# Every other weight chunk of the last down projection: low parts by an accumulating DMA in place of a VectorE subtraction

## The chip, the cores and the metric

One core of one Trainium2 chip runs the whole program. The metric is device time in microseconds (us) of one execution, the median of several runs of the same kernel. The core has a matrix engine (TensorE, PE in the rows, with its weight loads as PEld), VectorE (DVE), ScalarE (ACT), GpSimd (POOL), SyncE (SP), and 16 DMA engines that all queues share. SP and ACT hand their transfers to hardware queues (q1 and q10 in the profile); transfers that POOL issues go through a software queue (q0).

## The reference

Two transformer blocks run one after the other on a sequence of 256 positions with 1024 channels, all in float32. The first has a recurrent branch and an attention branch and a feed-forward part with a short convolution; the second has windowed attention, latent attention and a gated feed-forward part. Only the very end of the second block matters here:

```python
    h = rmsnorm_2(x, ffn_norm_g[l])
    x = x + (jax.nn.silu(h @ w_gate[l]) * (h @ w_up[l])) @ w_down[l]
    return rmsnorm_2(x, final_norm_g)
```

The last product, of a 256 x 2816 activation and the 2816 x 1024 matrix `w_down`, is what this document calls the last down projection. The addition of `x`, the final norm and the store follow it.

## The kernel before

**Split products.** Float32 accuracy on TensorE is had by splitting both operands. A value `w` is stored as a high part `wh`, which is `w` rounded to the narrower float32r type, and a low part `wl = w - wh`. A product takes three matmuls: activation high by weight high, activation low by weight high, activation high by weight low.

**Weight chunks.** All weights arrive in chunks of 128 partitions by up to 2048 columns. `produce()` makes one: SP loads it into a tile `wt`, ScalarE copies it into `wh` (the copy rounds), and VectorE subtracts to get `wl`. The pool `wp` has three buffers for each of `wt`, `wh` and `wl`, and `chunk()` keeps production two chunks ahead of use (`LOOK = 2`). From the second block's `w2_ukv` on, a chunk is loaded and split in two halves of 1024 columns (`cuts`), so that each chunk is two loads of 512 KB, two ScalarE copies and two VectorE subtractions.

**The last down projection.** `w2_down` has 11 chunks (d0 to d10 below; in the rows of the trace the digits in a tensor's name are left out, so it shows as in_w_down). Each chunk holds two blocks of 128 input rows (`k`), each 1024 columns wide, so a chunk's first half serves `k = 0` and its second half `k = 1`. Four PSUM banks (`o`, two token halves by two column halves) collect the result. For each chunk, each `k` and each `o` there are three matmuls of 512 columns, two of which read `wh` and the third `wl`: 24 matmuls a chunk. Chunk d9 is held back and done together with d10, bank by bank, so that the banks finish one after the other:

```python
        held += [(o, c, k, W) for k in range(2) for o in range(4)]
        if c == KH - 2:
            continue
        for o, c_, k, (wh, wl) in sorted(held, key=lambda x: x[0] if c == KH - 1 else 0):
```

**Order.** The program's order is not the order of the text. `Scheduler` collects all operations with a modelled cost, and list-schedules them: at each step the engine that can start first takes its available operation of the lowest index, and the result is emitted as one sequence (`emit`, the line 333 that all rows carry). Loads on every queue share one modelled "DMA" engine. The semaphores come from the tile framework: a reader waits for the tile's writer, and a new tile in a buffer waits until the last reader of the old tile is done. So the load of chunk c+3 into a `wt` buffer waits for the last reader of chunk c in that buffer, and the ScalarE copy into `wh` of chunk c waits for the last matmul that reads the `wh` of chunk c-3.

POOL computes nothing in this stage; it issues only five transfers in the whole program, the last two of them `final_g`.

Of the kernel before, what the change touches and what calls it, by code (L numbers as in the profile page):

```python
# [9 lines left out]
F32 = mybir.dt.float32  # L10
F32R = mybir.dt.float32r
BF16 = mybir.dt.bfloat16
AF = mybir.ActivationFunctionType
ALU = mybir.AluOpType
# [321 lines left out]
class Engines:  # L336
# [5 lines left out]
    def act(self, out, in_, func, **kw):  # L342
        n = max(out.n, in_.n)
        cost = (0.053 if in_.tile.psum else 0.093) + n / 1200.0
        cost += 0.09 * sum(isinstance(kw.get(k), View) for k in ("scale", "bias")) + (0.1 if "accum_out" in kw else 0.0)
        return self.sch.add("ACT", self.nc.scalar.activation, cost, (out, in_, func), kw, table=SETS.get(func))
# [16 lines left out]
    def dma(self, queue, out, in_):  # L363
        v = out if isinstance(out, View) else in_
        cost = v.shape[0] * v.n * 4 / 360e3
        self.sch.add(f"DMA", getattr(self.nc, queue).dma_start, cost, (out, in_), {}, lag=1.2)

    def memset(self, out, value):
        self.sch.add("DVE", self.nc.vector.memset, 0.1, (out, value), {})

# [31 lines left out]
def _build(ctx, tc, sch, A, out, order, used):  # L402
# [17 lines left out]
    V = Engines(sch, nc)  # L420
    act = V.act
# [60 lines left out]
    def produce():  # L482
        i = state["next"]
        name, idx = order[i]
        n = A[name].shape[-1]
        wt = wp.tile([P, 2048], F32, tag="wt")
        wh = wp.tile([P, 2048], F32R, tag="wh")
        wl = wp.tile([P, 2048], F32R, tag="wl")


        cuts = [0, n // 2, n] if i < 4 or i >= fine else [0, n]
        for a, b in zip(cuts, cuts[1:]):
            V.dma("sync", wt[:, a:b], A[name][idx][:, a:b])
            act(wh[:, a:b], wt[:, a:b], AF.Copy)
            V.tensor_sub(wl[:, a:b], wt[:, a:b], wh[:, a:b].bitcast(F32))
        ready[i] = (wh, wl)
        state["next"] = i + 1

    def chunk(name, idx):
        i = len(used)  # L500
        used.append((name, idx))
        if order is None:
            t = wp.tile([P, 2048], F32R, tag="wh")
            return t, t
        assert order[i] == (name, idx)
        while state["next"] <= min(i + LOOK, len(order) - 1):
            produce()
        return ready.pop(i)
# [874 lines left out]
```

## Time and profile before

| what | value |
| --- | --- |
| median of 3 runs | 808.87 us (808.72 to 810.1) |
| the profiled execution's own time | 809.6 us |
| its span, first to last instruction | 807.8 us |
| granted TensorE clock, mean | 0.999 |
| busy in the span | PE 796.9, PEld 684.3, DVE 598.4, ACT 522.8, POOL 3.0 us |
| all DMA, mean rate over the span | 175 GB/s |

The span is what the profiler's records cover; the execution's own time is a little longer. Engine shares are averages over stages of different kinds. A matmul's recorded duration overlaps with the next one's, so that the pitch between starts, and not the recorded duration, says how long a row of matmuls takes.

### The profile page before, as it was taken

How to read it: one execution, taken by the hardware profiler on the slowest of the kernel's cores; microseconds unless marked ns; L12 is line 12 of the kernel's file. 1: busy time of each engine (PE TensorE's matmuls, PEld its weight loads, DVE VectorE, ACT ScalarE, POOL GpSimd, SP SyncE). 2: the span in 40 equal slices, each digit the busy share in tenths (PEclk: the TensorE clock that was granted, in tenths of full speed). 3: DMA queues.
4: the chain of work that ended last, by engine and by line, in shares of the span. 5: the costliest groups of instructions: out<-in, count | busy, mean ns of one | idle time of the engine just before them, and what ended most of it. 6: DMA issues, size and time to landing. Idle time of an engine off the chain costs nothing.

```text
span 807.8 us, 11604 instructions
## 1 busy us (share of the span) xinstructions
PE 796.9 (99%) x4414; PEld 684.3 (85%) x4414; DVE 598.4 (74%) x999; ACT 522.8 (65%) x898; POOL 3.0 (0%) x9
## 2 busy tenths in 40 slices
PE   9999999999999999999999999999999999999996
PEld 6888888888888888888888888888888888888885
DVE  6777869977779798888656776666789887877443
ACT  7979889955445766666444667766746765555332
POOL 0000000000000000000000000000000000000000
PEclk9999999999999999999999999999999999999999
DMA  8853444565554455444556544423445665565631
GB/s 293 308 195 105 157 162 166 181 209 172 194 200 172 176 185 207 172 176 144 179 181 227 206 162 134 156 87 123 157 157 170 200 203 183 183 194 176 204 104 53
DMA packets 31260, 141.57 MB, mean 175 GB/s; under 512 B 3490, under 2 KB 5284, under 8 KB 23140
## 3 DMA queue, kind: packets, MB, share of 16 engines
q1 hardware_dynamic: 30228, 138.62, 50.6%
q0 software_dynamic: 400, 1.31, 0.5%
q10 hardware_dynamic: 576, 0.89, 0.3%
q8 instruction: 35, 0.57, 0.3%
q14 instruction: 21, 0.17, 0.1%
HBM read 139.76 MB, written 1.05 MB: 174 GB/s over the span
## 4 chain that ended last, share of the span: by engine, by line
PE 95%; ACT 2%; DMA 1%; DVE 1%; SPq 0%; issue 0%; DVEq 0%; ACTq 0%
PE b_banks L333 95%; DMA wt_wp<-in_w_q 1%; DMA u_up<-in_w_k 1%; ACT t_tp L333 1%; ACT wh_wp L333 1%; DVE wl_wp L333 0%; SPq L333 0%; DVE t_tp L333 0%; ACT pr_ap L333 0%; DVE u_up L333 0%; DVE pr_ap L333 0%; ACT k_cp L333 0%; DVEq L1378 0%; DVE k_cp L333 0%; DVE s_sp L333 0%
## 5 line engine op out<-in xcount | busy, mean ns | idle before, releaser
L333 PE MATMUL b_banks<-r_rp,wh_wp 128*128 128x512 f32 x1584 | 549.8, 398 | 0.0
L333 PE MATMUL b_banks<-r_rp,wl_wp 128*128 128x256 f32 x1584 | 414.5, 281 | 0.0
L333 DVE TENSOR_TENSOR wl_wp<-wt_wp,wh_wp 128x1024 fp32r<-128x1024 f32 (+4 forms) x187 | 298.8, 1611 | 79.4 <-ACT wh_wp L333 78.8
L333 PEld LDWEIGHTS b_banks<-r_rp,wh_wp 128*128 128x128 f32 x1584 | 285.6, 188 | 52.1
L333 PEld LDWEIGHTS b_banks<-r_rp,wl_wp 128*128 128x128 f32 x1584 | 298.3, 189 | 17.2
L333 ACT ACTIVATE wh_wp<-wt_wp 128x1024 fp32r<-128x1024 f32 (+4 forms) x187 | 252.1, 1368 | 72.0 <-PE b_banks L333 59.5
L333 ACT ACTIVATE t_tp<-b_banks 128x256 f32<-128x256 f32 (+1 forms) x180 | 68.8, 386 | 154.0 <-PE b_banks L333 153.9
L333 PE MATMUL b_banks<-wh_wp,r_rp 128*128 128x512 f32 (+2 forms) x472 | 146.1, 388 | 0.0
L333 PEld LDWEIGHTS b_banks<-wh_wp,r_rp 128*128 128x128 f32 x472 | 88.0, 188 | 15.9
L333 DVE TENSOR_TENSOR t_tp<-b_banks,t_tp 128x256 f32<-128x256 f32 (+1 forms) x160 | 61.4, 399 | 42.4 <-ACT t_tp L333 40.6
L333 PE MATMUL b_banks<-wl_wp,r_rp 128*128 128x512 f32 (+2 forms) x236 | 91.4, 387 | 0.4 <-DVE wl_wp L333 0.3
L333 PEld LDWEIGHTS b_banks<-wl_wp,r_rp 128*128 128x128 f32 x236 | 44.3, 188 | 9.6 <-DVE wl_wp L333 1.7
L333 DVE TENSOR_TENSOR t_tp<-t_tp,u_up 128x512 f32<-128x512 f32 x50 | 34.2, 686 | 2.3 <-ACT t_tp L333 1.5
L333 ACT ACT_TABLE_LOAD x26 | 33.4, 1283 | 1.2 <-PEq L1372 0.7
L333 DVE TENSOR_TENSOR t_tp<-t_tp,t_tp 128x512 f32<-128x512 f32 (+1 forms) x46 | 25.8, 564 | 5.7 <-ACT t_tp L333 5.3
L333 DVE SCALAR_TENSOR_TENSOR t_tp<-k_cp,k_cp,t_tp 128x256 f32<-128x256 f32 x68 | 28.3, 478 | 0.0
L333 DVE TENSOR_TENSOR r_rp<-t_tp,r_rp 128x512 fp32r<-128x512 f32 x34 | 23.2, 687 | 4.2 <-ACT r_rp L333 3.5
L333 DVE TENSOR_TENSOR u_up<-b_banks,t_tp 128x256 f32<-128x256 f32 x32 | 13.1, 421 | 16.8 <-ACT t_tp L333 16.8
L333 ACT ACTIVATE r_rp<-t_tp 128x512 fp32r<-128x512 f32 x34 | 21.2, 626 | 6.6 <-DVE t_tp L333 6.1
L333 DVE TENSOR_TENSOR u_up<-b_banks,u_up 128x256 f32<-128x256 f32 (+1 forms) x37 | 14.6, 437 | 9.6 <-PE b_banks L333 9.5
L333 ACT ACTIVATE pr_ap<-pr_ap,s_sp 128x128 f32<-128x128 f32 (+1 forms) x48 | 21.3, 447 | 0.0
L333 ACT ACTIVATE r_rp<-u_up,k_cp 128x256 fp32r<-128x256 f32 x32 | 14.9, 500 | 8.5 <-DVE u_up L333 5.2
(93 smaller groups left out, 470.5 us busy)
## 6 DMA issues: line engine op xcount, KB each, us to landing
wt_wp<-in_w_g SPq DMA_DIRECT2D x12, 1024.0 KB, 4.7
wt_wp<-in_w_up SPq DMA_DIRECT2D x11, 1024.0 KB, 4.7
wt_wp<-in_w_gate SPq DMA_DIRECT2D x11, 1024.0 KB, 4.8
wt_wp<-in_w_down SPq DMA_DIRECT2D x16, 704.0 KB, 4.1
wt_wp<-in_w_gate SPq DMA_DIRECT2D x22, 512.0 KB, 4.4
wt_wp<-in_w_up SPq DMA_DIRECT2D x22, 512.0 KB, 4.1
wt_wp<-in_w_down SPq DMA_DIRECT2D x22, 512.0 KB, 4.1
wt_wp<-in_w_x SPq DMA_DIRECT2D x4, 1024.0 KB, 4.8
```

The costliest lines, as they stand in the source:

```text
L333: op.fn(*[get(a) for a in op.args], **{k: get(v) for k, v in op.kw.items()})
```

## The change

The condition picks chunks d1, d3, d5, d7 and d9. For each half of these, ScalarE writes minus the rounded value into `wl` (a second copy, with scale -1), and a DMA issued by GpSimd then adds `wt` into `wl` in place; the VectorE subtraction is gone for them. Chunks with even numbers are made as before. The new operation has a modelled cost and a modelled delay of 2.0 us in the scheduler, on the same modelled "DMA" engine as the loads.

```diff
+    def dma_add(self, out, in_):
+        cost = out.shape[0] * out.n * 4 / 360e3
+        self.sch.add("DMA", self.nc.gpsimd.dma_start, cost, (out, in_), dict(accum_op=ALU.add), lag=2.0)
+
...
             V.dma("sync", wt[:, a:b], A[name][idx][:, a:b])
             act(wh[:, a:b], wt[:, a:b], AF.Copy)
-            V.tensor_sub(wl[:, a:b], wt[:, a:b], wh[:, a:b].bitcast(F32))
+            if name == "w2_down" and idx % 2:
+
+                act(wl[:, a:b], wt[:, a:b], AF.Copy, scale=-1.0)
+                V.dma_add(wl[:, a:b], wt[:, a:b])
+            else:
+                V.tensor_sub(wl[:, a:b], wt[:, a:b], wh[:, a:b].bitcast(F32))
```

## Rows read from the trace of the kernel before

**Rows 1.** The page: busy time of each engine; the chain that ended last.

```profile
PE 796.9 (99%) x4414; PEld 684.3 (85%) x4414; DVE 598.4 (74%) x999; ACT 522.8 (65%) x898; POOL 3.0 (0%) x9
...
PE 95%; ACT 2%; DMA 1%; DVE 1%; SPq 0%; issue 0%; DVEq 0%; ACTq 0%
```

**Rows 2.** The chain of waits from 735 us on: start, length, what.

```profile
734.89 66.72 PE b_banks L333 x303
```

**Rows 3.** Timeline, PE, 741 to 802: start, length, instructions.

```profile
741.59 0.62 PE L333 MATMUL b_banks<-wh_wp,r_rp 128*128 128x512 f32 x2
742.04 0.39 PE L333 MATMUL b_banks<-wl_wp,r_rp 128*128 128x512 f32 x1
...
747.03 0.62 PE L333 MATMUL b_banks<-wh_wp,r_rp 128*128 128x512 f32 x2
...
790.55 0.62 PE L333 MATMUL b_banks<-wh_wp,r_rp 128*128 128x512 f32 x2
...
801.21 0.39 PE L333 MATMUL b_banks<-wl_wp,r_rp 128*128 128x512 f32 x1
```

**Rows 4.** Timeline, ACT, 736 to 787; in brackets idle time before and its releaser.

```profile
736.47 2.00 ACT L333 ACTIVATE wh_wp<-wt_wp 128x1024 fp32r<-128x1024 f32 x2
738.37 0.62 ACT L333 ACTIVATE t_tp<-t_tp 128x512 f32<-128x512 f32 x1
739.01 1.28 ACT L333 ACT_TABLE_LOAD   x1
...
741.09 0.39 ACT L333 ACTIVATE t_tp<-b_banks 128x256 f32<-128x256 f32 x1 [0.59 <-PE b_banks L333]
...
743.96 0.63 ACT L333 ACTIVATE r_rp<-t_tp 128x512 fp32r<-128x512 f32 x1
747.05 2.01 ACT L333 ACTIVATE wh_wp<-wt_wp 128x1024 fp32r<-128x1024 f32 x2 [2.46 <-issue]
...
779.64 2.01 ACT L333 ACTIVATE wh_wp<-wt_wp 128x1024 fp32r<-128x1024 f32 x2 [3.43 <-PE b_banks L333]
785.09 2.01 ACT L333 ACTIVATE wh_wp<-wt_wp 128x1024 fp32r<-128x1024 f32 x2 [3.43 <-PE b_banks L333]
```

**Rows 5.** Timeline, DVE, the subtractions of d3, d9 and d10.

```profile
748.15 2.36 DVE L333 TENSOR_TENSOR wl_wp<-wt_wp,wh_wp 128x1024 fp32r<-128x1024 f32 x2 [1.92 <-ACT wh_wp L333]
...
780.74 2.36 DVE L333 TENSOR_TENSOR wl_wp<-wt_wp,wh_wp 128x1024 fp32r<-128x1024 f32 x2 [3.08 <-ACT wh_wp L333]
786.18 2.36 DVE L333 TENSOR_TENSOR wl_wp<-wt_wp,wh_wp 128x1024 fp32r<-128x1024 f32 x2 [3.08 <-ACT wh_wp L333]
```

**Rows 6.** Tile wt, 742 to 803: durations ns, minimum, median, maximum; landing in us.

```profile
L333 ACT ACTIVATE wh_wp<-wt_wp x18: 1044/1052/1061, 742.1 to 786.1; 128x1024 fp32r<-128x1024 f32 x18
L333 DVE TENSOR_TENSOR wl_wp<-wt_wp,wh_wp x18: 1216/1218/1226, 743.3 to 787.3; 128x1024 fp32r<-128x1024 f32 x18
...
DMA to landing us min/median/max: 3.9/4.1/4.9
```

**Rows 7.** Waits of SP's queue, 717 to 775: total us, times, longest.

```profile
SPq L333 <- DVE wl_wp L333: 50.2, 11, 4.7
```

**Rows 8.** Page and view of DMA issues: count, KB each, median us to landing.

```profile
wt_wp<-in_w_uq SPq DMA_DIRECT2D x4, 288.0 KB, 2.9
...
u_up<-in_final_g POOLq DMA_DIRECT2D x2, 256.0 KB, 3.0
...
u_up<-in_cbsb POOLq DMA_DIRECT2D x1, 256.0 KB, 4.5
```

**Rows 9.** Timeline, POOL: its last transfer.

```profile
560.77 0.54 POOL L333 DMA_DIRECT2D u_up<-in_final_g  x1 [11.30 <-PE b_banks L333]
```

**Rows 10.** Windows: busy PE, PEld, DVE, ACT, POOL; clock, DMA share, GB/s.

```profile
747.00:758.00 11.00, 11.00 (x50) 9.10 (x49) 4.72 (x4) 4.14 (x5) 0.00 (x0) 1.00 0.65 203
...
769.00:780.00 11.00, 11.00 (x50) 9.11 (x49) 4.72 (x4) 4.14 (x5) 0.00 (x0) 1.00 0.48 170
780.00:791.00 11.00, 11.00 (x50) 9.10 (x49) 4.72 (x4) 3.67 (x4) 0.00 (x0) 1.00 0.00 0
```

## The prediction

> **What bounds the kernel now.** I read the page first: PE is busy for 796.9 of 807.8 us, and the chain that ended last is 95% PE [rows 1]. A busy PE is not a PE at its peak, so I then read the chain in order of time: from 734.89 us on, one unbroken piece of 66.72 us of matmuls leads to 801.61, past which only the tail of the final norm is left [rows 2]. No wait for a weight chunk stands in it. The change touches this stretch alone, so the question is whether a low part ever comes late enough to break it.
>
> The PE timeline gives the due times [rows 3]. The last down projection begins at 741.59 with d0, d1 begins at 747.03, so a chunk takes 5.44 us, 0.227 us for each of its 24 matmuls. The third matmul of a chunk is the first that reads `wl`, 0.45 us after the chunk's start (742.04 after 741.59). The second half of `wl` is first read 12 matmuls later, at 2.72 + 0.45 = 3.17 us. For d9, which is interleaved with d10 from 790.55 on, the second half comes after three matmuls only, at 0.68 + 0.45 = 1.13 us.
>
> The ACT and DVE timelines give the times of production. ScalarE's copies for d3 begin at 747.05, with the start of d1; those for d9 at 779.64 and for d10 at 785.09 keep the step of 5.44 us, and the releaser is PE [rows 4]. This is the buffer rule: chunk c waits for the last matmul of c-3, which is the start of c-2. Let T be the start of ScalarE's work for a chunk; its first matmul then comes at T + 10.88. Each of the two copies costs 1.05 us with a pitch of 0.96 (two take 2.01), the first subtraction starts 1.10 after its copy started, and both are done by 750.51, T + 3.46 [rows 4, 5]. VectorE's work is thus ready 7.9 us before its use, and VectorE is idle more than half of this stage, 4.72 us busy in 11 [rows 10].
>
> **The change, part by part.**
>
> *Removed:* ten subtractions of 1218 ns, 12.2 us of VectorE [rows 6]. They end 7.9 us ahead of their use, so their removal gives 0.
>
> *Added on ScalarE:* ten copies of 1.05 us [rows 6]. An odd chunk then occupies ScalarE for about 4 x 0.96 + 0.1 = 3.9 us of its 5.44 instead of 2.0; before d9 and d10 it sat idle for 3.43 us [rows 4]. Cost 0, covered by that idle time. One place is tighter: d1 is made at 736.47, among the work of the gated part. Silu at 738.37 moves by 1.9 us to about 740.3, the table load behind it from 739.01 to 740.9, and the eviction due at 741.09 starts at about 742.4, 1.3 us late, since 0.59 us of idle time is used up [rows 4]. What waits for it: the copies of d2 (from 742.07 to about 743.4; their matmuls start at 752.47, two chunks after 741.59) and the split of the last activation tile (743.96 to about 745.3; only d10 reads it, after 790.55). Cost 0; without that cover it would be 1.3 us.
>
> *Added on POOL and the DMA engines:* ten in-place additions of 512 KB. POOL issued its last transfer at 560.77, in 0.54 us [rows 9]; nothing stands ahead of the additions on its queue, and behind each stands only the next. Order within a chunk: copy, minus-copy, addition, and the same for the second half. The minus-copy ends at the second pitch, so the first addition is issued at about T + 0.96 + 1.10 = T + 2.06 and the second at T + 3.98. Call the time from issue to landing L. Against the due times (T + 10.88 plus 0.45, 3.17, or 1.13):
>
> - first half: L up to 10.88 + 0.45 - 2.06 = 9.27 us (d1, which starts its copies at 736.47 for a first `wl` matmul at 747.48: 8.95);
> - second half: up to 10.07 us;
> - second half of d9: up to 10.88 + 1.13 - 3.98 = 8.03 us, the tightest.
>
> The trace shows no accumulating DMA and no transfer from SBUF to SBUF, so L is bounded by the nearest rows. A 256 KB load from POOL took 3.0 us, and 512 KB from SP in this stage 4.1; on SP 288 KB took 2.9 [rows 6, 8]. From 288 to 512 KB it is 1.2 us, or 2.7 us for each 512 KB more; the POOL path costs 0.3 us above that line. The addition reads two operands: L = 4.1 + 0.3 + 2.7 = 7.1 us, which I take, as an estimate. Lower end: 3.0 us, the POOL row itself. Upper end: the slowest POOL load, 4.5 us for 256 KB [rows 8], for each of the four 256 KB that an addition reads, 18 us. At 7.1 the tightest due time holds with 0.9 us left, the others with 1.9 or more. Cost 0.
>
> What a late addition would cost follows from the same times. A stall in chunk c puts off the start of c+1 and of c+2, while c+2's copies started with c; so the stall is also room for c+2. For one L everywhere, d1, d5 and d9 pay and d3 and d7 do not: (L - 8.95) + (L - 9.27) + (L - 8.03) = 3L - 26.25 us. At the upper end this is 27.8 us, at the lower end nothing. L = 9.3 us is the point from which 0.2% is lost.
>
> Only a page has a price for the addition itself: the Trainium skill, "Collectives: The Full Stack", section "The bandwidth ceiling: the fold count and why AG ≠ RS ≠ AR", puts an add at half the rate of a copy because it reads two sources, at about 31 GB/s a DMA engine for a copy. By that, 16 engines would need an estimated 2.1 us to move 512 KB, and the sum would be 0 as well; no trace here shows it.
>
> *Moved:* the release of `wt`. SP's queue now waits for VectorE's subtractions, 11 times in this stage, 50.2 us [rows 7]; after odd chunks it will wait for the second addition. For odd c the loads of c+3 go out at T + 3.98 + L, about T + 11.1 where it was T + 3.5, and land by about T + 15.7 with two loads in a row. ScalarE wants them at the start of c+1, T + 16.3. So they are just in time, and late loads have another 7.9 us before PE notices. Queued behind them on SP are the loads of c+4, wanted at T + 21.8. Cost 0. With the cover gone (L beyond 13) they would add to the stalls.
>
> **Sum.** 0 against the profiled execution's 809.6 us (span 807.8, 1.8 us around it). That execution lies 0.7 us above the median of 808.87 and inside the runs' 808.72 to 810.1; I predict 808.9. About 0.2%, 1.6 us, is what a measurement of this kernel can tell from no change.
>
> **The rivals.**
>
> *A. The addition takes longer than its room (slower).* Place: the first `wl` matmul of d1 and d5 and the second half of d9. Decides from L = 9.3. If reading and writing back were two POOL transfers in a row at the slowest POOL pace, 4.5 us and 1.4 more (the slope above) for 512 KB, L is 11.8, and 3L - 26.25 gives 9.2 us: 818.0. For it: no row shows such an operation, and POOL loads reached 4.5. Against: the two final_g loads took 3.0 [rows 8], and the margin at my estimate is 0.9 us for d9 and 1.9 or more for the others. Chance 0.10.
>
> *B. The DMA engines become the bound.* From 747 to 758 they were busy 65% at 203 GB/s [rows 10]: 312 GB/s when busy, 1.68 us for 512 KB. From the first addition at 738.5 on, 14 loads (d4 to d10) take 23.5 us, and ten additions that read twice 33.6 us; that ends at 795.6, where the last addition is due at 791.68: 3.9 us, 812.8. Against: the loads stop early, with the share at 0.48 from 769 and 0.00 from 780 to 791 [rows 10], and a busy share counts waiting for HBM too, which a transfer inside SBUF does not have. Chance 0.08.
>
> *C. VectorE holds up POOL's issue.* Were each addition to wait out the pair of subtractions of an even chunk, 2.36 us [rows 5], L would be 9.5 and the time 811.0. Against: the pair for d10 runs from 786.18, when the additions of d9 (issued at about 781.7 and 783.6) are under way. The Trainium skill, "SBUF — State Buffer", section "SBUF: two separate sides", says that GpSimd cannot write descriptors while VectorE runs an operation in a two-port mode. No run here shows this yet. Chance 0.03.
>
> *D. Faster by over 0.2%.* PE would have to run its matmuls closer than 0.227 us because VectorE reads less. In 780 to 791, with no DMA at all, PE did the same 50 matmuls in 11 us as in 747 to 758 [rows 10], so neighbours do not seem to set its pitch. I price it at 2 us, 806.9. Chance 0.04.
>
> **How the numbers follow.** No change: 0.75. A and B and C are slower: 0.21, faster 0.04. The range goes from 807.4, below the runs' lowest by their spread, to 814.0, above B and C; outside it are A and half of D, some 0.12, and a little of the main case.
>
> **What would show it.** Right: VectorE has ten subtractions fewer, ScalarE ten copies more, PE's piece of the chain from 735 on is still about 66.7 us, d1 still follows d0 after 5.44 us, and the additions land within 8.0 us. Wrong: a PE wait released by a POOL transfer on `wl`, first at d1 or in d9's second half; or SP loads that land in more than 6 us and copies of even chunks that wait for them.

## The result, and the profile after

The changed kernel took 816.4 us (median of four runs, 813.91 to 818.02) against 808.93 for the kernel before on the same chip: a ratio of 1.0089, with a 95% interval of 1.0069 to 1.0108. It is slower by 0.9%, where no change was forecast and the range ended at 814.0.

The profiled execution has a span of 815.4 us, 7.6 more than before. The page: busy time by engine, and the chain that ended last; these answer to [rows 1].

```profile
PE 798.3 (98%) x4414; PEld 685.0 (84%) x4414; DVE 586.9 (72%) x989; ACT 532.0 (65%) x908; POOL 11.7 (1%) x19
...
PE 86%; DMA 5%; issue 4%; ACT 2%; DVE 2%; SPq 0%; POOL 0%; DVEq 0%; POOLq 0%; ACTq 0%
```

VectorE did ten instructions fewer and ScalarE ten more, so the change did what it says. But the chain is no longer PE alone. The chain in order of time, which answers to [rows 2], has lost its unbroken piece of matmuls:

```profile
750.81 9.63 DMA wl_wp<-wt_wp
760.44 0.02 SPq L333
760.46 0.03 issue
760.49 6.31 DMA wt_wp<-in_w_down
...
776.88 9.02 DMA wl_wp<-wt_wp
785.91 0.04 issue
785.95 23.21 PE b_banks L333 x94
```

It reads: the second addition of d3 (issued at 750.81) lands after 9.63 us; SP's queue, which stood waiting for it, issues a load; and the first addition of d7 (issued at 776.88) lands after 9.02 us, when PE goes on at once. Between that load's landing (766.8) and 776.88 the chain shows almost nothing but 9.99 us of "issue": it does not follow ScalarE there, whose rows further down fill this gap.

The PE timeline, those matmuls that read `wl`, where a normal step from one to the next is 0.68 us, as in [rows 3]:

```profile
771.06 0.39 PE L333 MATMUL b_banks<-wl_wp,r_rp 128*128 128x512 f32 x1
773.44 0.50 PE L333 MATMUL b_banks<-wl_wp,r_rp 128*128 128x512 f32 x1 [1.54 <-DMA wl_wp<-wt_wp]
774.25 0.39 PE L333 MATMUL b_banks<-wl_wp,r_rp 128*128 128x512 f32 x1
...
781.06 0.39 PE L333 MATMUL b_banks<-wl_wp,r_rp 128*128 128x512 f32 x1
785.95 0.80 PE L333 MATMUL b_banks<-wl_wp,r_rp 128*128 128x512 f32 x1 [4.05 <-DMA wl_wp<-wt_wp]
787.39 0.63 PE L333 MATMUL b_banks<-wl_wp,r_rp 128*128 128x512 f32 x1
788.68 0.63 PE L333 MATMUL b_banks<-wl_wp,r_rp 128*128 128x512 f32 x1
789.70 0.40 PE L333 MATMUL b_banks<-wl_wp,r_rp 128*128 128x512 f32 x1
...
808.76 0.39 PE L333 MATMUL b_banks<-wl_wp,r_rp 128*128 128x512 f32 x1
```

The loss can be added up from these starts. The second half of d5 comes 1.70 us late (771.06 to 773.44 less 0.68) and the step after it is 0.13 too long. The first half of d7 comes 4.21 us late (781.06 to 785.95 less 0.68). Then three steps take 3.75 us where they should take 2.04, 1.71 more. Together 7.75 us. The last `wl` matmul starts at 808.76 instead of 801.21, 7.55 later, though the first, at 741.60, was 0.44 sooner than before; the 0.24 still missing lie mostly at d3, where the two steps that end at 758.81 are too long. The long matmuls behind the second wait are the clock: the window from 780 to 791 below has a mean grant of 0.84, and within it the microsecond from 786.90 on has 0.50, the lower level, 1.2 GHz. There a matmul that takes 0.39 us elsewhere took 0.63, and a step 1.29 instead of 0.68.

Windows, with the columns of [rows 10]:

```profile
747.00:758.00 11.00, 11.00 (x49) 8.83 (x48) 2.36 (x2) 6.08 (x7) 1.70 (x2) 1.00 1.03 260
...
780.00:791.00 11.00, 6.95 (x24) 5.33 (x23) 1.82 (x2) 4.27 (x5) 1.72 (x2) 0.84 1.03 224
...
786.90:787.90 1.00, 1.00 (x4) 0.74 (x3) 0.00 (x0) 0.00 (x0) 0.46 (x1) 0.50 1.00 197
```

The DMA engines, busy 65% from 747 to 758 before, are now full there, and again from 780 to 791, where they had nothing to do before. The queues and the issues from 735 to 800 us (packets, MB, share of sixteen engines; count, KB, median us to landing):

```profile
q0 software_dynamic: 1440, 5.24, 42.6%
q1 hardware_dynamic: 2302, 8.38, 39.6%
...
wt_wp<-in_w_down SPq DMA_DIRECT2D x14, 512.0 KB, 6.3
wl_wp<-wt_wp POOLq DMA_DIRECT2D x10, 512.0 KB, 8.3
```

Ten additions took 0.426 x 65 = 27.7 us of all sixteen engines, 2.8 us each. The loads' queue took 25.7 us for 8.38 MB, which is what sixteen loads carry (14 were issued in this window, and what was still under way from before counts too): 1.6 us each, or 22.5 for the 14. A load lands after 6.3 us, not 4.1 [rows 6]. The tile `wl` (durations in ns; landing in us, minimum, median, maximum):

```profile
L333 ACT ACTIVATE wl_wp<-wt_wp x10: 1039/1042/1059, 735.5 to 785.2; 128x1024 fp32r<-128x1024 f32 x10
L333 POOL DMA_DIRECT2D wl_wp<-wt_wp x10: 845/854/899, 736.9 to 786.5; - x10
...
DMA to landing us min/median/max: 5.0/8.3/11.8
```

The waits of SP's queue, which answer to [rows 7], and ScalarE's timeline for d6 and d7:

```profile
SPq L333 <- DMA wl_wp<-wt_wp: 44.6, 5, 11.6
```

```profile
768.12 1.06 ACT L333 ACTIVATE wh_wp<-wt_wp 128x1024 fp32r<-128x1024 f32 x1 [6.78 <-DMA wt_wp<-in_w_down]
773.63 2.01 ACT L333 ACTIVATE wh_wp<-wt_wp 128x1024 fp32r<-128x1024 f32 x2 [4.45 <-DMA wt_wp<-in_w_down]
775.55 1.04 ACT L333 ACTIVATE wl_wp<-wt_wp 128x1024 fp32r<-128x1024 f32 x1
```

ScalarE, which used to wait for PE [rows 4], now waits for loads. The row at 773.63 holds the second half of d6 and the first of d7, in that order: d7 stands behind d6 on ScalarE's queue. Its minus-copy starts at 775.55, its addition goes out at 776.88 and lands at 785.9. SP began no issue between 746.96 and 760.49, and then four loads within 2.3 us, beside the two additions of d5. In the order in which the kernel emits them, these are the first half of d7, both halves of d6 and the second half of d7. The last two, issued at about 761.4 and 762.8, landed 12.3 and 11.9 us later (view of DMA issues):

```profile
wt_wp<-in_w_down SPq DMA_DIRECT2D x1, 512.0 KB, 12.3
...
wt_wp<-in_w_down SPq DMA_DIRECT2D x1, 512.0 KB, 11.9
```

So the first half of d7 was there at 766.8, in time for its due start at 768.6, and waited on ScalarE's queue for the second half of d6.

### The profile page after: what moved, and what is told of

It is laid out like the page before. It is cut to its first block, busy times and chain, and to the rows that moved or that the text cites. A ratio compares the mean times of both kernels' runs of the same rounds, so it can differ in the third digit from the quotient of the medians.

```text
span 815.4 us, 11629 instructions
## 1 busy us (share of the span) xinstructions
PE 798.3 (98%) x4414; PEld 685.0 (84%) x4414; DVE 586.9 (72%) x989; ACT 532.0 (65%) x908; POOL 11.7 (1%) x19
## 4 chain that ended last, share of the span: by engine, by line
PE 86%; DMA 5%; issue 4%; ACT 2%; DVE 2%; SPq 0%; POOL 0%; DVEq 0%; POOLq 0%; ACTq 0%
PE b_banks L333 86%; DMA wl_wp<-wt_wp 2%; DMA wt_wp<-in_w_down 1%; DMA wt_wp<-in_w_q 1%; DVE wl_wp L333 1%; ACT t_tp L333 1%; ACT wh_wp L333 1%; DMA u_up<-in_x 1%; SPq L333 0%; DVE t_tp L333 0%; POOL wl_wp L333 0%; ACT pr_ap L333 0%; DVE u_up L333 0%; DVE pr_ap L333 0%; ACT k_cp L333 0%
## 5 line engine op out<-in xcount | busy, mean ns | idle before, releaser
L333 DVE TENSOR_TENSOR wl_wp<-wt_wp,wh_wp 128x1024 fp32r<-128x1024 f32 (+4 forms) x177 | 287.2, 1634 | 97.6 <-ACT wh_wp L333 96.9
```

The source lines that it names most:

```text
L333: op.fn(*[get(a) for a in op.args], **{k: get(v) for k, v in op.kw.items()})
```

## The experiments

After this reading three theories stood. **Theory 1, transfer:** additions and loads together are too much for the DMA engines, so additions land late, whoever waits for what. **Theory 2, release:** an addition keeps `wt` until it lands, the next loads go out late, and the lateness runs through the queues of SP and ScalarE into the next odd chunk. **Theory 3, order:** the scheduler's modelled cost put one load of d7 ahead of those of d6, which made d6 late. Of the kernels below, plain_copy, f32_out and hbm_hold emit the loads in this swapped order too; hbm_addend, model_free, act_only, first_half, wl_first and only_d5 emit them in the old order, d6 before d7; no_loads has none of them. All ratios are against the kernel before on the same chip, with 95% intervals.

**hbm_addend**

```diff
-                V.dma_add(wl[:, a:b], wt[:, a:b])
+                V.dma_add(wl[:, a:b], A[name][idx][:, a:b])
```

> The additions read the weight a second time from HBM and no longer from wt, so that wt is free after the two ScalarE copies; everything else as in the changed kernel, the loads again in the order d6, d7. Theory 1 (transfer: the sixteen DMA engines are too slow for additions and loads together, whoever waits for what): the bytes are the same, L stays at 8 to 10 us, PE still waits for wl, 811 to 816 us. Theory 2 (release: loads are held back because an addition keeps wt, and the lateness passes through SP's and ScalarE's queues to the next odd chunk): loads go out as before the change, 808.5 to 810.5 us with no PE wait over 0.5 us. Theory 3 (order: the scheduler put a load of d7 ahead of those of d6): like theory 2, since the order is restored too.

810.49 us, ratio 1.0013 (1.0003 to 1.0022): most of the loss is gone. The view of DMA issues (the last number is the median landing), then PE's waits and SP's (total us, times, longest):

```profile
wl_wp<-in_w_down POOLq DMA_DIRECT2D x10, 512.0 KB, 8.3
```

```profile
PEld b_banks L333 <- DMA wl_wp<-in_w_down: 1.2, 2, 0.9
PE b_banks L333 <- DMA wl_wp<-in_w_down: 0.5, 1, 0.5
```

```profile
SPq L333 <- ACT wl_wp L333: 18.2, 4, 5.3
```

The additions land as late as in the changed kernel (median 8.3 in both), and still PE hardly waits; SP waits for ScalarE's copies and no longer for the landing. The DMA engines were no less full than in the changed kernel (a share of 0.95 from 747 to 791, against 0.92). ScalarE waited for no load. So additions as long as these, beside loads, cost about 1 us when no load is held back, and theory 1 does not account for the rest. This kernel also restores the order, so theories 2 and 3 both fit it.

**model_free**

```diff
-        cost = out.shape[0] * out.n * 4 / 360e3
-        self.sch.add("DMA", self.nc.gpsimd.dma_start, cost, (out, in_), dict(accum_op=ALU.add), lag=2.0)
+        cost = 0.0
+        self.sch.add("POOL", self.nc.gpsimd.dma_start, cost, (out, in_), dict(accum_op=ALU.add), lag=0.0)
```

> Only the modelled cost of the addition is changed (0 on an engine of its own, no delay), which brings the SP queue back to the order d6, d7; the additions still keep wt. Theory 3: the waits of PE go, 808.5 to 810.5 us. Theories 1 and 2: the same transfers and the same holds, 812 to 818 us, PE waits of 4 us or more in all.

816.24 us, ratio 1.0084 (1.0054 to 1.0113), as slow as the changed kernel with the loads in their old order. Theory 3 falls. PE stood for 5.5 us in all, as against 5.6 in the changed kernel; the row of PEld shows the same stops as its weight loads saw them, and is not to be added. ScalarE waits for loads as well:

```profile
PEld b_banks L333 <- DMA wl_wp<-wt_wp: 6.8, 3, 2.6
PE b_banks L333 <- DMA wl_wp<-wt_wp: 5.5, 3, 2.2
ACT wh_wp L333 <- DMA wt_wp<-in_w_down: 23.0, 9, 4.2
```

The chain in order of time shows the release at work:

```profile
761.86 12.94 DMA wl_wp<-wt_wp
...
776.66 8.57 DMA wt_wp<-in_w_down
...
786.30 1.05 ACT wl_wp L333
...
790.13 9.19 DMA wl_wp<-wt_wp
799.37 11.64 PE b_banks L333 x43
```

The second addition of d5 lands at 774.8. Only then does SP send the loads of d8, and behind them that of d9, which lands at 785.2; ScalarE makes the copies of d9, and its second addition lands when PE has already stood for 2.17 us. The order of instructions on every computing engine and of the loads is that of hbm_addend, so the two kernels differ in two things: where the addend comes from, and that `wt` is kept until an addition has landed.

**plain_copy**

```diff
-        self.sch.add("DMA", self.nc.gpsimd.dma_start, cost, (out, in_), dict(accum_op=ALU.add), lag=2.0)
+        self.sch.add("DMA", self.nc.gpsimd.dma_start, cost, (out, in_), {}, lag=2.0)
```

> The DMA copies wt into wl without adding (the subtraction of the high part is left out, so wl holds the whole weight); the instruction order of every engine is that of the changed kernel. Theory 1: half of what each transfer reads is gone, the software queue's time for ten transfers falls from 27.7 us of all engines to about 15, L to 5 or 6 us, and the time to 808.5 to 811. Theory 3: the order is still wrong, 812 us or more. Theory 2: release follows L, so in between, 809 to 813.

809.18 us, ratio 0.9999 (0.9990 to 1.0009). The software queue and the issues:

```profile
q0 software_dynamic: 1440, 5.24, 22.0%
...
wl_wp<-wt_wp POOLq DMA_DIRECT2D x10, 512.0 KB, 5.2
```

Ten plain copies took 0.220 x 65 = 14.3 us of all engines, 1.4 each, half of what the additions took. With the same instruction order and the same hold on `wt`, only shorter by some 3 us, nothing is lost. So a hold as such is not enough, and the wrong order, still there, costs nothing by itself.

**no_loads**

```diff
-        wt = wp.tile([P, 2048], F32, tag="wt")
+        again = name == "w2_down" and idx > 3
+        wt = state["wt"] if again else wp.tile([P, 2048], F32, tag="wt")
+        state["wt"] = wt
...
-            V.dma("sync", wt[:, a:b], A[name][idx][:, a:b])
+            if not again:
+                V.dma("sync", wt[:, a:b], A[name][idx][:, a:b])
```

> Chunks d4 to d10 are made from the wt tile of d3 again (their loads are left out), so that the additions run with no load beside them. If an addition is long by itself: L 8 us or more and 811 us or more. If it is long because it shares the engines with loads (theory 1), or if the trouble is the release or the order of loads (theories 2 and 3): L 5 to 6.5 us and 808.5 to 810 us, no PE wait for wl.

809.01 us, ratio 0.9998 (0.9989 to 1.0008). The same view:

```profile
q0 software_dynamic: 1440, 5.24, 40.9%
...
wl_wp<-wt_wp POOLq DMA_DIRECT2D x10, 512.0 KB, 5.1
```

An addition with no load beside it lands after 5.1 us, though it takes the engines as long as before (0.409 x 65 = 26.6 us for ten). The length of 8.3 comes from sharing with loads.

**hbm_hold** puts back the hold on top of hbm_addend.

```diff
                 V.dma_add(wl[:, a:b], A[name][idx][:, a:b])
+                if b == n:
+                    sch.add("POOL", nc.gpsimd.tensor_tensor, 0.2, (small(1), wt[:, b - 1 : b], wl[:, b - 1 : b].bitcast(F32), ALU.add), {})
```

> The addend comes from HBM as in hbm_addend, but a tiny POOL addition that reads one column of wt and one of wl is put behind each pair of additions, so that wt stays held until the second addition has landed, as in the changed kernel. If the hold is the cause (theory 2): the time goes back to 813 to 818 us with PE waits of 3 us or more. If it is where the addend is read from, or the saturated engines alone (theory 1): 809.5 to 811 us, as hbm_addend.

818.24 us, ratio 1.0112 (1.0096 to 1.0129): the whole loss is back. ScalarE's waits and PE's, then SP's:

```profile
ACT wh_wp L333 <- DMA wt_wp<-in_w_down: 19.4, 9, 5.6
PEld b_banks L333 <- DMA wl_wp<-in_w_down: 9.1, 6, 2.1
PE b_banks L333 <- DMA wl_wp<-in_w_down: 6.6, 6, 1.7
```

```profile
SPq L333 <- POOL s_sp L333: 33.7, 3, 12.4
```

Same additions, same source, same bytes; without the hold 1.0013, with it 1.0112. But the hold is not all that the edit put back. The loads go out in the swapped order again, and the tiny addition waits on POOL's own queue, so that the next chunk's additions wait behind it, here for d7:

```profile
773.52 0.18 POOL L333 TENSOR_TENSOR s_sp<-wt_wp,wl_wp 128x1 f32<-128x1 f32 x1 [12.04 <-DMA wl_wp<-in_w_down]
774.07 0.86 POOL L333 DMA_DIRECT2D wl_wp<-in_w_down  x1 [0.37 <-issue]
```

The first additions of d5, d7 and d9 went out 0.9, 0.8 and 1.4 us later than their minus-copies allow (1.33 us after a minus-copy starts, as in the changed kernel), so part of the 1.1% may be POOL's queue; this run can't tell how much. It does answer what model_free against hbm_addend left open: with the addend from HBM and `wt` held, ScalarE waits 19.4 us for loads where it waited for none. No pair of runs differs in the hold alone; the two pairs together, and the chain of model_free, speak for it.

**act_only**

```diff
                 act(wl[:, a:b], wt[:, a:b], AF.Copy, scale=-1.0)
-                V.dma_add(wl[:, a:b], wt[:, a:b])
-            else:
-                V.tensor_sub(wl[:, a:b], wt[:, a:b], wh[:, a:b].bitcast(F32))
+            V.tensor_sub(wl[:, a:b], wt[:, a:b], wh[:, a:b].bitcast(F32))
```

> The minus-copies on ScalarE are made, and VectorE then subtracts over them as before the change; no addition by DMA. All three theories take the copies to be free: 808.3 to 809.8 us, no PE wait. If ScalarE's 3.9 us per odd chunk cost something: 810.5 us or more.

808.68 us, ratio 0.9996 (0.9987 to 1.0005). The ten copies on ScalarE are free.

**first_half**

```diff
-            if name == "w2_down" and idx % 2:
+            if name == "w2_down" and idx % 2 and a == 0:
```

> Only the first half of each odd chunk gets its low part by DMA, the second by VectorE: five additions, issued at T + 2.1, so wt is held some 3 to 4 us less and the DMA engines have 13.5 us less work. Theories 1 and 2 together: L 5 to 8.5 us, no load later than ScalarE wants it by more than 2 us, 808.5 to 810 us. If any one addition in a chunk is enough to break the row: 811 us or more.

808.88 us, ratio 0.9996 (0.9987 to 1.0006); the five additions land after 4.4 to 6.2 us. Half the additions cost nothing: the loss is not a price that every addition pays.

**f32_out**

```diff
-                V.dma_add(wl[:, a:b], wt[:, a:b])
+                V.dma_add(wl[:, a:b].bitcast(F32), wt[:, a:b])
```

> The destination is named as plain float32, so that the addition needs no conversion to float32r; the order of all engines is that of the changed kernel. If the conversion makes the addition long: the software queue's time for ten falls well below 27 us of all engines, L to 5 to 6, time 808.5 to 811 us. If the second read does (theory 1 with plain_copy's result): unchanged, 813 to 818 us, L 8 us or more.

815.13 us, ratio 1.0074 (1.0051 to 1.0096). The software queue:

```profile
q0 software_dynamic: 1440, 5.24, 41.1%
```

The conversion to float32r does not make the addition long; 0.411 x 65 = 26.7 us, as with it. (Its median landing in the one profiled execution was 6.5 us, under the 8 expected; that execution had a span of 811.3, the shortest of the slow kernels' profiled executions. The landings vary between executions as the times do.)

**wl_first**

```diff
+        odd = name == "w2_down" and idx % 2
+        for a, b in halves if odd else []:
+            V.dma("sync", wt[:, a:b], A[name][idx][:, a:b])
+            act(wl[:, a:b], wt[:, a:b], AF.Copy, scale=-1.0)
+            V.dma_add(wl[:, a:b], wt[:, a:b])
+        for a, b in halves:
...
             act(wh[:, a:b], wt[:, a:b], AF.Copy)
```

> In odd chunks ScalarE makes both minus-copies first and the two high copies after them, so that the additions go out about 0.96 and 1.9 us sooner; the work is the same. Theory 2 as a loop (odd chunk's addition lands, then the load, then the copy of the odd chunk two further on, 25.8 us round where PE needs one every 21.8): 1.9 us off the round and off the hold, a part of the loss comes back, 809.5 to 814 us. If the saturated engines alone set the time (theory 1): no change, 814 to 818.

816.62 us, ratio 1.0084 (1.0067 to 1.0100): no gain, a miss. ScalarE's timeline for d3 shows that the edit did only half of what it was for: the scheduler still put one high copy ahead, so that only the second addition moved, by one copy's pitch.

```profile
747.85 1.06 ACT L333 ACTIVATE wh_wp<-wt_wp 128x1024 fp32r<-128x1024 f32 x1 [1.37 <-issue]
748.81 1.99 ACT L333 ACTIVATE wl_wp<-wt_wp 128x1024 fp32r<-128x1024 f32 x2
```

The next loads then went out at 761.1, 13.2 us after the start of d3's copies; in the changed kernel it was 760.5 and 13.9. That 0.7 us brought nothing back. The result neither proves nor refutes the round of 25.8 us that I had put into the expectation, and that number stays an argument.

**only_d5**

```diff
-            if name == "w2_down" and idx % 2:
+            if name == "w2_down" and idx == 5:
```

> Additions for d5 alone, so that two stand beside an ordinary stream of loads and no second pair follows. Theory 2: one held wt makes one late pair of loads, covered by the 7.9 us ahead of PE: 808.3 to 809.8 us, no PE wait, L 5.5 to 7.5. If a single held chunk is enough: 811 us or more.

809.15 us, ratio 0.9999 (0.9989 to 1.0008); the two additions landed after 4.5 and 6.4 us. Beside an ordinary stream of loads an addition is well inside its room. Landings of over 8 us were seen only in kernels that have loads and add both halves of every odd chunk.

## Why the prediction was wrong

**What held.** VectorE's ten subtractions were worth nothing (plain_copy does without them, at a ratio of 0.9999), and ScalarE's copies cost nothing (act_only). POOL issued at once: 845 to 899 ns each, with no sign of VectorE holding it up (the issue at 778.78 ran into d8's subtractions, which start at 779.47, and took 0.85 us like the rest), so rival C did not come about. The Trainium skill's rule on GpSimd and VectorE's two-port modes ("SBUF — State Buffer", section "SBUF: two separate sides") was not tested by any run here. Rival A put the stall at d1, d5 and d9; PE waited at d5 and d7. That its 818.0 lies near the measured 816.4 is luck: it needs an L of 11.8 for every addition. One of the prediction's signs of being wrong did come, and it names the path: loads that land in more than 6 us, and copies of an even chunk (d6) that wait for them.

**The term that was mis-sized: L.** I took 7.1 us from rows in which loads share with loads alone. Alone an addition lands after 5.1 us; in the changed kernel after 8.3, and up to 11.8. At 8.3 for every addition the prediction's own due times give 0.3 us, at d9, where PE did not wait. Rival B priced the engines' work at 33.6 us for the additions and 23.5 for the 14 loads; 27.7 and 22.5 were measured. Its argument that a load from HBM counts as busy for longer than a transfer inside SBUF holds, but in a small size: in plain_copy 512 KB took the engines 1.69 us from HBM and 1.43 inside SBUF. The Trainium skill ("Collectives: The Full Stack", section "The bandwidth ceiling: the fold count and why AG ≠ RS ≠ AR") says that an add runs at half a copy's rate for its two reads. Rows come near the half, though they do not show the reason: 26.6 us for ten additions against 14.3 for ten copies, a ratio of 1.86. The 2.1 us estimated from its rate is low; 2.7 was measured. But L by itself is the smaller part: hbm_addend has the same L and loses 0.13%.

**The step that failed: the moved release of `wt`.** It said that loads of c+3 "are just in time, and late loads have another 7.9 us before PE notices", and priced the whole at nothing up to an L of 13. Two things in it were wrong. First, it let the loads land in 4.6 us. Loads held back until the additions land go out together and meet the next odd chunk's additions: in the changed kernel SP sent nothing for 13.5 us and then four, of which two took about 12. Secondly, the 7.9 us belong to even chunks alone. Behind the late even chunk, on ScalarE's queue (and, in the old order of loads, on SP's too), stands the next odd chunk, whose addition has only its own 9.27 less L. The copies of d7 were due with the start of d5, at 768.6, and its first minus-copy a pitch later, at 769.5. It came at 775.55, 6.0 us late; PE's own stop of 1.8 us at d5 gave back a part, and with an L of 9.0 the rest became PE's 4.05 us. hbm_addend against model_free and against hbm_hold shows that additions of this length cost 0.13% where `wt` is free and 0.8 to 1.1% where it is held, each pair with the further differences named above; plain_copy, first_half and only_d5 show that with a shorter transfer or fewer of them the same hold costs nothing. It takes both.

**What I had not priced at all:** the clock. After its wait at d7 PE ran some matmuls at 1.2 GHz and lost another 1.7 us, over a fifth of the whole. The swap in SP's order was not foreseen either, but it cost nothing that model_free or plain_copy could show.

What stays open is how the 7.6 us split between a late d7 and a slow DMA in any one execution: the changed kernel's own runs spread over 4.1 us, and only one of them has a profile.

## What to carry to other kernels

When an operation moves from an engine to a DMA, price not only when its result is due but when its *source buffer* comes free: the next load waits for the landing, and with three buffers that goes round to the same operation four chunks on (here from d3 to d7). Slack at one chunk is no cover for the chunk queued behind it on an in-order queue; compute the room of the tightest chunk that can inherit the delay. And take a transfer's time from rows in which the engines are as full as they will be: the same addition landed in 5.1 us alone and in 8.3 beside the loads.

## What the runs showed of the hardware

An in-place addition of 512 KB inside SBUF took the sixteen engines 2.7 us, a plain copy of the same tile 1.4; POOL's issue of it took 0.85 us against 0.53 for the copy. Whether the addend came from SBUF or HBM made no difference to the median landing (8.3 in both) and little to the engines' time (2.8 and 3.0 us each beside loads); nor did the conversion to float32r make one to the engines' time. And a PE wait of 4.05 us was followed by a granted clock of 0.50 and steps of up to twice the length, so that the wait cost 1.7 us more than its length.
